# One more pair of heads in flight in sliding-window attention, and the keys' PSUM work issued two to a bank

## The chip, the cores and the metric

The kernel runs on one core of a Trainium2 chip. The metric is the time on the device of one execution, in microseconds; lower is better. The engines that matter are TensorE (PE, with its weight loads as PEld), VectorE (DVE) and ScalarE (ACT). Each takes its own instructions strictly from its own program and waits on semaphores for the others; weights come from HBM through SyncE's DMA queue.

## The reference

The model is a decoder trunk of two layers for 256 tokens of width 2048: an RG-LRU layer, then a sliding-window attention layer with grouped queries, each followed by a SwiGLU. The change is in the second layer alone:

```python
def shared_kv(x, g, w_kv, k_g):
    h = rms_norm(x, g)
    k, v = jnp.split(h @ w_kv, 2, axis=-1)
    k = rms_norm(k.reshape(bsz, s, N_KV_HEADS, HEAD_DIM), k_g)
...
def attn_block(x, g, w_q, q_g, sinks, w_o, k_band, v_band):
    q = rms_norm((h @ w_q).reshape(bsz, s, N_KV_HEADS, GROUP, HEAD_DIM), q_g)
    scores = jnp.einsum("bnqhgd,bnkhd->bnhgqk", q, k_band) * (1.0 / math.sqrt(HEAD_DIM))
    scores = jnp.where(mask, scores, NEG_INF)
    probs = jax.nn.softmax(jnp.concatenate([scores, sink], axis=-1), axis=-1)[..., :-1]
    out = jnp.einsum("bnhgqk,bnkhd->bnqhgd", probs, v_band)
    return x + out.reshape(bsz, s, N_HEADS * HEAD_DIM) @ w_o
```

There are 32 query heads of 64 values and 4 key/value heads; a token sees its own block of 128 tokens up to itself and the part of the block before that lies within 128 tokens.

## The kernel before

**Projections.** Everything is held transposed: features on the partitions, the 256 tokens along the free axis. A weight matrix is cut into tiles of 256 rows by 512 columns. Each tile is a *block* of work (a job): SyncE loads it (`raw`), ScalarE rounds it to `hi` (L243), VectorE takes the rest `lo` (L244), and TensorE multiplies hi by both halves of the activation and lo by the upper half (L281), normally 24 instructions of 256 columns; where two halves are done in one of 512 columns a block has 21. Tiles are loaded four blocks ahead and split three blocks ahead. `group` runs the blocks that add up to four output tiles in four PSUM banks.

**Background work.** All the rest (norms, softmax, copies) is written as generators, which `run_bg` steps between half blocks ("ticks") as far as a budget of VectorE and ScalarE time allows; a `yield n` asks for n ticks' pause. When a block needs an activation that is not yet made, `need` steps the generators until it is there. At most four PSUM banks (`MISC`) are out for background work. The recording layer then places the instructions of each engine, so the order on an engine is not exactly that of the code; the order shown below is the final one.

**Keys.** `kv` projects keys and values. Its task normalises the keys: L704 squares them, L712 sums the squares per head on TensorE (two matmuls, a bank each), L718 to L722 scale, L730 copies each of the four heads' keys to both halves of the partitions through a matmul (a bank each, in turn), and L733 splits the copy into hi and lo as `kd`.

**Attention.** `attn` projects queries in four groups; each group's task makes four *pairs* of heads ready (L959), 16 pairs in all. `pairs` handles them in *turns*, at least `VISIT` = 3 ticks apart. A turn issues on TensorE: the values of pair A (L804, L806: probabilities times V), the six transposes of pair B's probabilities (L814), and the scores of a new pair (L825). Then ScalarE copies the transposes out of PSUM (L895, L896) and the values are split into `at` (L901, by L347 and L348; this is what the output projection reads), and the new pair's softmax follows (`softmax`: VectorE's masked reduction L837, ScalarE's exponentials L851, VectorE's scaling L859). Helpers hold the actual calls, so in the profile ScalarE's work shows as L107 and VectorE's scaling as L125. A pair is thus scored in one turn, transposed in the next and multiplied with the values in the one after.

**Output projection.** L965 multiplies by w_o with `late` = 2: the first two groups run as first six blocks of group 0, first six of group 1, then the last two of each. Block c reads the outputs of pairs 2c and 2c + 1, so pair 11 is first read in the sixth block and pair 15 in the fourteenth.

Of the kernel before, what the change touches and what calls it, by code (L numbers as in the profile page):

```python
# [15 lines left out]
ALU = mybir.AluOpType  # L16

P = 128
D = 2048
T = 256  # L20
DFF = 5632
ND = D // P
NH = DFF // P
HD = 64
EPS = 1e-6
# [10 lines left out]
K_ONE, K_BLK, K_SEL0, K_SEL1, K_ID = 0, 128, 256, 384, 512  # L36
# [12 lines left out]
class Trunk:  # L49
# [470 lines left out]
    def lru(self, gains, rn):  # L520
# [80 lines left out]
        def recur(v):  # L601

            A = lambda s: s[:, 0:T]
            B = lambda s: s[:, T:2 * T]
# [74 lines left out]
    def kv(self, xs, r, gains):  # L679
        nc, con, par = self.nc, self.con, self.par  # L680
        st = {}
        self.kvs = []
        w = self.d["kv"]
        self.kd = [Val() for _ in range(4)]
        self.v = [Val() for _ in range(2)]

        def done(ps):
            k0 = [self.pull((p, False, p)) for p in ps[:2]]
            for b in range(2):
                self.a(self.v[b].ap, ps[2 + b][:, 0:T])  # L690
                self.free_bank(ps[2 + b])

            def task():
                while not self.rv[r].ready:
                    yield 1
                rs = self.rstd[r][:, 0:T]
                for b in range(2):
                    self.ts(self.v[b].ap, self.v[b].ap, self.rstd[r][:, T + b:T + b + 1], None, ALU.mult)
                    self.v[b].ready = True
                    yield  # L700
                sl = [self.slot(F32) for _ in range(2)]
                for j in range(2):
                    self.tt(k0[j], k0[j], rs, ALU.mult)
                    self.a(sl[j][:, 0:T], k0[j], AF.Square)  # L704
                    yield
                yield 1
                p2 = []
                for j in range(2):
                    while not self.room():
                        yield 1  # L710
                    p2.append(self.mbank())
                    nc.tensor.matmul(p2[j][:, 0:T], con[:, K_BLK:K_BLK + P], sl[j][:, 0:T],  # L712
                                     start=True, stop=True)
                yield 1
                for j in range(2):
                    A, B = (sl[j][:, h * T:(h + 1) * T] for h in range(2))
                    m, t = self.nm[:, 0:T], self.nt[:, 0:T]
                    self.ts(m, p2[j][:, 0:T], 1.0 / HD, EPS, ALU.mult, ALU.add)  # L718
                    self.free_mbank(p2[j])
                    self.rsqrt(B, m, t)  # L720
                    self.tt(k0[j], k0[j], B, ALU.mult)
                    self.ts(A, k0[j], par[:, C_GK:C_GK + 1], par[:, C_GQ:C_GQ + 1], ALU.mult, ALU.mult)  # L722
                    yield
                yield 1
                for h in range(4):
                    while not self.room():
                        yield 1
                    p = self.mbank()
                    sel = (K_SEL0, K_SEL1)[h % 2]
                    nc.tensor.matmul(p[:, 0:T], con[:, sel:sel + P], sl[h // 2][:, 0:T],  # L730
                                     start=True, stop=True)
                    yield 1
                    self.split_act(self.kd[h].ap, p[:, 0:T])  # L733
                    self.free_mbank(p)
                    self.kd[h].ready = True
                    yield
                for s in sl:
                    self.free(s)
                for s in k0:
                    self.free_half(s)  # L740
            self.spawn(task())

        for c in range(8):
            def mm(hi, lo, c=c):
                if c == 0:
                    st["ps"] = [self.bank() for _ in range(4)]
                    self.DVE_TICK, self.ACT_TICK, self.SPARE = self.LATER

                    for h in range(4):
                        self.kd[h].ap = self.slot()  # L750
                        self.kvs.append(self.kd[h].ap)
                    s = self.slot(F32)
                    self.kvs.append(s)
                    for b in range(2):
                        self.v[b].ap = s[:, b * T:(b + 1) * T]

                    def more():
                        for k in range(ND):
                            self.gained(k, gains)
                            yield  # L760
                    self.spawn(more())
                ps = st["ps"]
                k0 = 2 * c
                x2 = [self.need(xs[k0 + kt]) for kt in range(2)]
                for f in range(2):
                    for kt in range(2):
                        for high, q in ((1, 0), (1, T), (0, 0)):
                            w0 = (hi if high else lo)[:, kt * 512 + f * P:kt * 512 + f * P + P]
                            nc.tensor.matmul(ps[f][:, 0:T], w0, x2[kt][:, q:q + T],
                                             start=k0 + kt == 0 and high > q, stop=k0 + kt == ND - 1 and not high)  # L770
                self.half_tick()
                for b in range(2):
                    for kt in range(2):
                        k = 2 * c + kt
                        wh, wl = (q[:, kt * 512 + 256:kt * 512 + 512] for q in (hi, lo))
                        xh, xl = (x2[kt][:, q * T + b * P:q * T + b * P + P] for q in range(2))
                        o = ps[2 + b][:, 0:T]
                        nc.tensor.matmul(o, xh, wh, start=k == 0, stop=False)
                        nc.tensor.matmul(o, xh, wl, start=False, stop=False)
                        nc.tensor.matmul(o, xl, wh, start=False, stop=k == ND - 1)  # L780
                for q in x2:
                    self.free(q)
                if c == 7:
                    done(ps)
            self.jobs.append((w[c], mm))

    def attn(self, xs, r, gains, rn):
        nc, con, par = self.nc, self.con, self.par
# [74 lines left out]
        def pairs():  # L863


            A = B = None
            n = 0
            while n < ND or A or B:
                new = None
                if todo and self.kd[todo[0][0] // 4].ready and self.v[0].ready and self.v[1].ready:  # L870
                    new = todo.popleft()
                    n += 1
                elif not (A or B):
                    yield 1
                    continue
                at_tick = self.tick
                count = 2 * bool(A or B) + 2 * bool(new)
                while self.misc + count > self.MISC or len(self.banks) < count or len(self.slots) < 5:
                    yield 1
                pt = [self.mbank() for _ in range(2)] if A or B else None  # L880
                ps = [self.mbank() for _ in range(2)] if new else None
                if A:
                    values(A[0], A[1], pt[1])
                    self.pe(900)
                if B:
                    transposes(B[1], pt)
                    self.pe(700)
                if new:
                    scores(new[0], new[1], ps)
                    self.pe(900)  # L890
                yield 1
                nextA = None
                if B:
                    s = [self.slot(F32) for _ in range(2)]
                    self.a(s[0], pt[0])  # L895
                    self.a(s[1][:, 0:T], pt[1][:, 0:T])  # L896
                    nextA = (B[0], s)
                    yield
                if A:
                    s = self.slot()  # L900
                    self.split_act(s, pt[1][:, T:2 * T])  # L901
                    at[A[0]].ap = s
                    at[A[0]].ready = True
                    yield
                for p in pt or ():
                    self.free_mbank(p)
                A, B = nextA, None
                if new:
                    sc = [self.slot(F32) for _ in range(2)]
                    yield from softmax(new[0], new[2], ps, sc)  # L910
                    B = (new[0], sc)
                yield max(1, at_tick + self.VISIT - self.tick)
            for q in self.kvs:
                self.free(q)
# [145 lines left out]
```

## Time and profile before

| what | before |
|---|---|
| median of three runs | 2011.34 us (2009.05 to 2012.57) |
| the profiled execution: its time | 2007.98 us |
| the profiled execution: its span | 2006.2 us |
| TensorE busy, matmuls | 1988.6 us |
| keys' sums and copies (L712, L730) on TensorE | 1041.4 to 1062.0 us |
| scores (L825) on TensorE | 1071.2 to 1215.3 us |
| values (L804, L806) on TensorE | 1083.6 to 1226.4 us |

A row of the groups of instructions reads: line, engine, operation, written<-read tiles, shape, xcount, then total busy time and mean ns of one, then the idle time ahead of them and who ended it. A row of who waited for whom reads: waiting engine, tile and line <- the one waited for, then us in all, times, longest. A row of the timeline reads: start, duration, instruction, count, and in brackets the idle time ahead of it. A row of the stretches reads: stretch, its length, then busy time (and count) of PE, PEld, DVE, ACT and POOL, granted clock, DMA share and GB/s.

### The profile page before, as it was taken

Reading aid. Unit: us, or ns where it says so; the run is one execution under the profiler, and the core shown is the slowest. Engines: PE = TensorE matmul, PEld = TensorE weight load, DVE = VectorE, ACT = ScalarE, POOL = GpSimd, SP = SyncE. Lnnn points to the kernel's source line nnn. Section 1 sums busy time; section 2 is a strip of 40 time slices with the busy share of each in tenths; the row PEclk is TensorE's granted clock in tenths of the full one; section 3 lists DMA queues with packets and bytes.
Section 4 is the critical chain, followed back from the end, with each engine's and each line's share of the span. In section 5 each row is a group of like instructions: output and inputs, shape, how many; then the busy total and the mean of one; then the engine's idle time right before and its main releaser. Section 6 shows DMA issues by size and latency. Waiting matters only on the chain. (4 is left out here: it accounts for less than half of the span.)

```text
span 2006.2 us, 40340 instructions
## 1 busy us (share of the span) xinstructions
PE 1988.6 (99%) x16843; PEld 1948.9 (97%) x16843; DVE 1275.2 (64%) x2043; ACT 1075.3 (54%) x1619; POOL 0.2 (0%) x4
## 2 busy tenths in 40 slices
PE   9999999999999999999999999999999999999999
PEld 9999999999999999999998889999999999999999
DVE  8989876566556555554677766665566566554443
ACT  7798755454445444443556665554454455444432
POOL 0000000000000000000000000000000000000000
PEclk9999999999999999999999999999999999999999
DMA  7655665666656566655653334656555656666663
GB/s 265 201 188 169 215 193 192 194 196 192 197 191 195 194 193 195 193 191 196 197 182 127 116 117 150 192 189 196 196 192 194 195 191 197 192 196 202 205 206 126
DMA packets 105014, 376.57 MB, mean 188 GB/s; under 512 B 11648, under 2 KB 13824, under 8 KB 104832
## 3 DMA queue, kind: packets, MB, share of 16 engines
q1 hardware_dynamic: 104544, 373.60, 57.6%
q8 instruction: 131, 2.15, 0.4%
q10 hardware_dynamic: 288, 0.40, 0.1%
q14 instruction: 51, 0.42, 0.1%
HBM read 371.86 MB, written 2.10 MB: 186 GB/s over the span
## 5 line engine op out<-in xcount | busy, mean ns | idle before, releaser
L281 PE MATMUL b<-s,hi 128*128 128x256 f32 (+1 forms) x10424 | 1428.2, 283 | 3.5 <-ACT s L107 1.9
L281 PEld LDWEIGHTS b<-s,hi 128*128 128x128 f32 x10424 | 1319.4, 188 | 31.8 <-ACT s L107 2.5
L244 DVE TENSOR_TENSOR lo<-raw,hi 128x1024 fp32r<-128x1024 f32 (+1 forms) x705 | 860.6, 1221 | 666.4 <-ACT hi L243 661.9
L243 ACT ACTIVATE hi<-raw 128x1024 fp32r<-128x1024 f32 (+1 forms) x705 | 745.7, 1059 | 775.6 <-PE b L281 743.0
L281 PE MATMUL b<-s,lo 128*128 128x256 f32 x5504 | 821.2, 276 | 0.0
L281 PEld LDWEIGHTS b<-s,lo 128*128 128x128 f32 x5504 | 714.8, 188 | 0.0
L107 ACT ACTIVATE t<-b 128x256 f32<-128x256 f32 x130 | 48.8, 384 | 59.4 <-PE b L281 38.3
L107 ACT ACTIVATE h<-h 128x256 f32<-128x256 f32 (+1 forms) x104 | 38.8, 375 | 20.9 <-DVE h L116 20.8
L107 ACT ACTIVATE s<-h 128x256 fp32r<-128x256 f32 (+1 forms) x106 | 42.7, 411 | 12.5 <-DVE h L116 10.1
L107 ACT ACTIVATE s<-s 128x256 f32<-128x256 f32 (+1 forms) x112 | 41.0, 417 | 5.5 <-DVE s L120 4.6
L116 DVE TENSOR_TENSOR h<-b,rstd 128x256 f32<-128x256 f32 x100 | 40.9, 414 | 0.0
L107 ACT ACTIVATE s<-x,par 128x256 fp32r<-128x256 f32 x80 | 37.9, 497 | 4.2 <-DVE x L116 3.3
L107 ACT ACT_TABLE_LOAD x31 | 39.8, 1283 | 0.5
L116 DVE TENSOR_TENSOR h<-h,rstd 128x256 f32<-128x256 f32 x94 | 39.0, 419 | 1.5
L116 DVE TENSOR_TENSOR h<-b,t 128x256 f32<-128x256 f32 x92 | 38.2, 417 | 0.0
L120 DVE SCALAR_TENSOR_TENSOR s<-x,par,s 128x256 fp32r<-128x256 f32 x80 | 36.7, 478 | 0.8 <-ACT s L107 0.8
L107 ACT ACTIVATE s<-b 128x256 f32<-128x256 f32 (+2 forms) x64 | 24.7, 435 | 23.0 <-PE b L814 16.7
L116 DVE TENSOR_TENSOR s<-h,s 128x256 fp32r<-128x256 f32 x88 | 36.5, 417 | 0.0
L116 DVE TENSOR_TENSOR h<-h,h 128x256 f32<-128x256 f32 x88 | 36.3, 415 | 0.1
L116 DVE TENSOR_TENSOR s<-s,s 128x256 fp32r<-128x256 f32 (+1 forms) x80 | 31.0, 417 | 5.9 <-ACT s L107 5.8
L837 DVE CUSTOM_DVE_ANT_0 s<-b,con,par 128x128 f32<-128x128 f32 x64 | 27.8, 472 | 6.3 <-PE b L825 6.1
L107 ACT ACTIVATE s<-s,h 128x128 f32<-128x128 f32 x64 | 28.2, 442 | 4.2 <-DVE h L125 4.2
(95 smaller groups left out, 554.5 us busy)
## 6 DMA issues: line engine op xcount, KB each, us to landing
raw<-in_ffn_in SPq DMA_DIRECT2D x352, 512.0 KB, 4.0
raw<-in_ffn_out SPq DMA_DIRECT2D x176, 512.0 KB, 4.2
raw<-in_lru_in SPq DMA_DIRECT2D x63, 512.0 KB, 3.8
raw<-in_lru_out SPq DMA_DIRECT2D x32, 512.0 KB, 3.8
raw<-in_w_q SPq DMA_DIRECT2D x32, 512.0 KB, 3.3
raw<-in_w_o SPq DMA_DIRECT2D x32, 512.0 KB, 3.4
raw<-in_gate SPq DMA_DIRECT2D x8, 512.0 KB, 4.1
raw<-in_kv SPq DMA_DIRECT2D x8, 512.0 KB, 3.3
```

The costliest lines, as they stand in the source:

```text
L107: self.nc.scalar.activation(out, in_, func, **kw)
L116: self.nc.vector.tensor_tensor(out, a, b, op)
L120: self.nc.vector.scalar_tensor_tensor(out, a, s, b, op0, op1)
L243: self.nc.scalar.activation(hi[:, q], raw[:, q], AF.Copy)
L244: self.nc.vector.tensor_tensor(lo[:, q], raw[:, q], hi[:, q].bitcast(F32), ALU.subtract)
L281: self.nc.tensor.matmul(ps[f][0][:, 0:c1 - c0], w, x2[k][:, c0:c1], start=ps[f][2] not in begun, stop=last and all(q[1] != f for q in todo ...
L837: nc.vector.tensor_tensor_reduce(sc[hh][:, c0:c1], ps[hh][:, c0:c1], con[:, K_MASK + c0:K_MASK + c1], rr[:, b * 8 + f * 2 + hh:b * 8 + f * ...
```

## The change

A third place C is put behind B: a pair that is scored goes to C, a turn later to B, and is transposed in the turn after that. So a pair takes four turns in place of three, one more pair is in flight, and `pairs` runs a turn longer. A turn now asks for six free slots of SBUF in place of five. For the keys, the two sums of squares share one PSUM bank; the four copies are issued together into two banks, two to a bank, after a pause of three ticks, and their splits follow one after another.

```diff
-                p2 = []
+                while not self.room():
+                    yield 1
+                p2 = self.mbank()
                 for j in range(2):
-                    while not self.room():
-                        yield 1
-                    p2.append(self.mbank())
-                    nc.tensor.matmul(p2[j][:, 0:T], con[:, K_BLK:K_BLK + P], sl[j][:, 0:T],
+                    nc.tensor.matmul(p2[:, j * T:j * T + T], con[:, K_BLK:K_BLK + P], sl[j][:, 0:T],
                                      start=True, stop=True)
...
+                yield 3
+                while self.misc + 2 > self.MISC or len(self.banks) < 2:
+                    yield 1
+                ps = [self.mbank() for _ in range(2)]
+                for h in range(4):
+                    sel = (K_SEL0, K_SEL1)[h % 2]
+                    nc.tensor.matmul(ps[h // 2][:, h % 2 * T:h % 2 * T + T], con[:, sel:sel + P], sl[h // 2][:, 0:T],
+                                     start=True, stop=True)
                 yield 1
                 for h in range(4):
-                    while not self.room():
-                        yield 1
-                    p = self.mbank()
-                    sel = (K_SEL0, K_SEL1)[h % 2]
-                    nc.tensor.matmul(p[:, 0:T], con[:, sel:sel + P], sl[h // 2][:, 0:T],
-                                     start=True, stop=True)
-                    yield 1
-                    self.split_act(self.kd[h].ap, p[:, 0:T])
-                    self.free_mbank(p)
+                    self.split_act(self.kd[h].ap, ps[h // 2][:, h % 2 * T:h % 2 * T + T])
+                    if h % 2:
+                        self.free_mbank(ps[h // 2])
...
-            A = B = None
+            A = B = C = None
             n = 0
-            while n < ND or A or B:
+            while n < ND or A or B or C:
...
-                elif not (A or B):
+                elif not (A or B or C):
...
-                while self.misc + count > self.MISC or len(self.banks) < count or len(self.slots) < 5:
+                while self.misc + count > self.MISC or len(self.banks) < count or len(self.slots) < 6:
...
-                A, B = nextA, None
+                A, B, C = nextA, C, None
                 if new:
                     sc = [self.slot(F32) for _ in range(2)]
                     yield from softmax(new[0], new[2], ps, sc)
-                    B = (new[0], sc)
+                    C = (new[0], sc)
```

In the changed kernel the lines of `attn` stand two further down: values are L806 and L808, transposes L816, scores L827.

The order of instructions moves at three places that matter below. The first is TensorE in an early turn. In these rows b0 to b7 are the PSUM banks, con_65 the constants (here the identity), and the s are slots; in the kernel before, the turn that does pair 0's values, pair 1's transposes (s39, s41 hold its probabilities) and pair 2's scores (into b5 and b6) stands so:

```order
L804 MATMUL b0_83<-s35_11811,s34_11072 64x256 x2
L806 MATMUL b0_83<-s40_11812,s34_11072 64x128 x2
...
L825 MATMUL b5_88<-s30_11068,s53_11649 128x256
L814 MATMUL b0_83<-con_65,s39_11816 128x128
L814 MATMUL b3_86<-con_65,s39_11816 128x128 x2
L814 MATMUL b0_83<-con_65,s41_11815 128x128
L814 MATMUL b3_86<-con_65,s41_11815 128x128 x2
L825 MATMUL b6_89<-s30_11068,s53_11649 128x256
```

and in the changed kernel the turn with pair 0's values, pair 1's transposes and pair 3's scores so:

```order
L806 MATMUL b5_88<-s41_11893,s34_11072 64x256 x2
L808 MATMUL b5_88<-s39_11894,s34_11072 64x128 x2
L816 MATMUL b5_88<-con_65,s40_11821 128x128
L816 MATMUL b0_83<-con_65,s40_11821 128x128 x2
L816 MATMUL b5_88<-con_65,s35_11820 128x128
L816 MATMUL b0_83<-con_65,s35_11820 128x128 x2
L827 MATMUL b6_89<-s30_11068,s31_11663 128x128
L827 MATMUL b7_90<-s30_11068,s31_11663 128x128
```

The transposes stood among the scores, behind nine of the twelve; now they stand between values and scores.

The second place is TensorE at the sixth block of w_o. Before, pair 11's values (into b4) stand two blocks and a half ahead of the block that reads its output, slot s10:

```order
L281 MATMUL b2_85<-s1_12466,hi2_77 128x256 x4
L804 MATMUL b4_87<-s39_12999,s34_11072 64x256 x2
L806 MATMUL b4_87<-s53_13000,s34_11072 64x128 x2
L281 MATMUL b7_90<-s1_12466,hi2_77 128x256 x4
...
L281 MATMUL b2_85<-s20_13003,hi1_76 128x256 x4
L281 MATMUL b7_90<-s20_13003,hi1_76 128x256 x4
L281 MATMUL b2_85<-s10_13067,hi1_76 128x256 x4
```

and now (values into b5, output in slot s33, with pair 13's twelve scores between):

```order
L281 MATMUL b0_83<-s49_13043,lo0_79 128x256 x2
L806 MATMUL b5_88<-s55_13110,s34_11072 64x256 x2
L808 MATMUL b5_88<-s26_13111,s34_11072 64x128 x2
L827 MATMUL b6_89<-s9_11071,s15_12920 128x128
...
L281 MATMUL b7_90<-s51_13114,hi1_76 128x256 x4
L281 MATMUL b0_83<-s51_13114,hi1_76 128x256 x4
L281 MATMUL b7_90<-s33_13167,hi1_76 128x256
L281 MATMUL b0_83<-s33_13167,hi1_76 128x256
L281 MATMUL b1_84<-s1_11984,hi2_77 128x256 x3
```

Values and reader have moved together, and the reader is followed by three matmuls of another block, put there ahead of the rest of s33's.

The third place is ScalarE's program at the same point. Before, the copy of pair 11's output from b4 stands ahead of three weight splits, the table load and the exponentials of pair 12 (h6 holds that pair's sums):

```order
L107 ACTIVATE s10_13067<-b4_87 128x256
L243 ACTIVATE hi2_77<-raw2_73 128x1024
L243 ACTIVATE hi3_78<-raw3_74 128x1024
L243 ACTIVATE hi0_75<-raw0_71 128x1024
L107 ACT_TABLE_LOAD
L107 ACTIVATE h6_101<-h6_101 128x4
```

and now (the output of pair 11 in s33, that of pair 10 in s51):

```order
L107 ACTIVATE s51_13114<-b4_87 128x256
L243 ACTIVATE hi0_75<-raw0_71 128x1024
L107 ACT_TABLE_LOAD
L107 ACTIVATE h6_101<-h6_101 128x4
L107 ACTIVATE s21_13117,h6_101<-s21_13117,h6_101 128x128
L107 ACTIVATE s21_13117,h6_101<-s21_13117,h6_101 128x256
L107 ACTIVATE s22_13118,h6_101<-s22_13118,h6_101 128x128
L107 ACTIVATE s22_13118,h6_101<-s22_13118,h6_101 128x256
L107 ACTIVATE s33_13167<-b5_88 128x256
```

The copy has moved from ahead of the split, the load and the exponentials to behind them.

More of the change, by code (lines that the diff above doesn't have):

```diff
@@ L717, in task @@
                     m, t = self.nm[:, 0:T], self.nt[:, 0:T]
-                    self.ts(m, p2[j][:, 0:T], 1.0 / HD, EPS, ALU.mult, ALU.add)
-                    self.free_mbank(p2[j])
+                    self.ts(m, p2[:, j * T:j * T + T], 1.0 / HD, EPS, ALU.mult, ALU.add)
+                    if j:
+                        self.free_mbank(p2)
                     self.rsqrt(B, m, t)
```

## The prediction

> **What bounds the kernel now.** First the page: its span, the busy row of TensorE and the granted clock.
>
> ```profile
> span 2006.2 us, 40340 instructions
> PE 1988.6 (99%) x16843; PEld 1948.9 (97%) x16843; DVE 1275.2 (64%) x2043; ACT 1075.3 (54%) x1619; POOL 0.2 (0%) x4
> PEclk9999999999999999999999999999999999999999
> ```
>
> TensorE is busy nearly all the time and its clock is never cut, so only time in which TensorE stands still, or work taken off it, can shorten the run. 2006.2 - 1988.6 = 17.6 us of standing still is all there is in the matmul records. So the second view is the table of who waited for whom, of matmuls (PE) and of weight loads (PEld), in the stretch 1035 to 1240 us in which the change works:
>
> ```profile
> PE b L814 <- DVE s L125: 9.7, 11, 1.0
> PEld b L814 <- DVE s L125: 12.2, 12, 1.3
> PEld b L825 <- issue: 2.5, 15, 0.2
> ```
>
> The only matmuls that stand still there are the transposes of the probabilities (L814): 11 times they wait for VectorE's last scaling of the softmax (L125), 9.7 us in all, and 12.2 us by the weight loads. The third view, TensorE's instructions in order of time, tells which figure is the loss:
>
> ```profile
> 1065.52 1.10 PE L281 MATMUL b<-s,lo 128*128 128x256 f32 x8
> 1066.46 1.57 PE L281 MATMUL b<-s,hi 128*128 128x256 f32 x12
> ...
> 1078.88 0.75 PE L281 MATMUL b<-s,hi 128*128 128x256 f32 x5
> 1080.60 0.88 PE L814 MATMUL b<-con,s 128*128 128x128 f32 x6 [0.98 <-DVE s L125]
> 1081.23 1.54 PE L281 MATMUL b<-s,hi 128*128 128x256 f32 x11
> ```
>
> Eight matmuls of 256 columns take 1066.46 - 1065.52 = 0.94 us from start to start, 0.1175 us each. The five from 1078.88 should thus have let the transposes start at 1079.47; they started at 1080.60. That is 1.13 us lost where the matmul record says 0.98, because the modelled end of a matmul overlaps what follows. 12.2 / 11 = 1.11 agrees with 1.13, so I take 12.2 us as the loss and keep 9.7 as its lower bound.
>
> The Trainium skill, page "Perfetto Trace Analysis", section "Identifying the Most-Contended Engine", says that matmul busy time is a poor measure for a pipelined TensorE and that the busy share of the weight loads should be read in its place. By the matmul wait alone the sum below would be 2.5 us smaller; the start times just read agree with the page.
>
> **The change, part by part.** *Transposes two turns behind.* Before, a turn transposes the pair whose scores stood one turn earlier; now it transposes the pair of two turns earlier. By the order of the changed kernel, pair 0 has 69 matmul rows of L281 between its scores and its transposes, where it had 50, and most later pairs more. The work between is a whole turn of other pairs, so all of VectorE's scalings for a pair are queued ahead of the next pair's last reduction. That takes away up to the whole loss: **-12.2 us** (bounds -9.7 and -12.2).
>
> What is late next? The tightest are pairs 0 and 4, the first of their groups.
>
> ```profile
> 1071.16 0.95 PE L825 MATMUL b<-s,s 64*128 64x128 f32 x12
> 1072.05 2.15 PE L281 MATMUL b<-s,hi 128*128 128x256 f32 x13
> ...
> L837 DVE CUSTOM_DVE_ANT_0 s<-b,con,par 128x128 f32<-128x128 f32 x32 | 13.0, 406 | 6.3 <-PE b L825 6.1
> L837 DVE DVE_READ_ACCUMULATOR2_ANT h<- 128x1 f32 x64 | 5.3, 83 | 0.0
> ```
>
> Pair 0's scores started at 1071.16 and its probabilities were ready at 1080.60, 9.44 us later. In the new order of VectorE one more score reduction of pair 1 stands ahead of pair 0's scalings, 0.406 + 0.083 = 0.49 us: ready after 9.93. TensorE gets there after two sets of scores (1072.05 - 1071.16 = 0.89 each), 69 rows of L281 of which three are 512 wide (so 72 x 0.1175 = 8.46) and two entries of 0.1 each: 10.4 us. The margin is 0.5 us for each of the two pairs. As VectorE can be a little late I put **+0.3 us** for both together (bounds 0 and 1.0).
>
> *A turn more at the end.* The output projection L965 reads the attention outputs in order; pairs now finish a turn later, while its blocks stand where they stood. In the order shown above, the values of pair 11 stood some 70 matmuls of L281 ahead of the ones that read them; now their block follows pair 11's values and pair 13's scores directly, with 8 matmuls between. And ScalarE's copy of that output (L347) now stands behind a weight split, a table load and the exponentials of pair 12. The trace has the same queue for the same pair in the old kernel:
>
> ```profile
> 1191.36 0.96 PE L825 MATMUL b<-s,s 64*128 64x128 f32 x12
> 1192.24 2.15 PE L281 MATMUL b<-s,hi 128*128 128x256 f32 x16
> ...
> 1194.48 1.06 ACT L243 ACTIVATE hi<-raw 128x1024 fp32r<-128x1024 f32 x1 [2.84 <-PE b L281]
> 1195.56 1.28 ACT L107 ACT_TABLE_LOAD   x1
> 1196.85 0.21 ACT L107 ACTIVATE h<-h 128x4 f32<-128x4 f32 x1
> ...
> 1198.72 1.04 ACT L243 ACTIVATE hi<-raw 128x1024 fp32r<-128x1024 f32 x1
> ```
>
> The split waits for TensorE to have read the buffer that it overwrites (16 matmuls from 1192.24 end their starts at 1194.12; it begins 0.36 us later), then come the load (1.28 us) and the exponentials, and ScalarE is free at 1198.72, 7.36 us after the start of pair 12's scores. The copy behind them and the values' own time:
>
> ```profile
> L107 ACT ACTIVATE s<-b 128x256 fp32r<-128x256 f32 x16 | 6.2, 388 | 3.6 <-PE b L806 3.6
> ...
> 1203.89 0.65 PE L804 MATMUL b<-s,s 128*64 128x256 f32 x4
> 1204.37 0.39 PE L806 MATMUL b<-s,s 128*64 128x128 f32 x4
> 1204.69 0.84 PE L825 MATMUL b<-s,s 64*128 64x128 f32 x9
> ```
>
> The copy ends at 7.36 + 0.39 = 7.75 us. TensorE, counted from the same start: pair 12's scores 0.89, 24 matmuls 2.82, an entry 0.1, values 1204.69 - 1203.89 = 0.80, pair 13's scores 0.89, 8 matmuls 0.94: 6.44 us. So it waits 7.75 - 6.44 = **+1.3 us** at this block (bounds: 0 if the split finds its buffer free earlier, 2.4 if one more split of 1.06 us stands in the way). VectorE's half of that output is wanted five matmuls later and follows within 0.5 us of the copy, which five matmuls (0.59 us) cover. At pair 15 the same thing happens without a softmax in the queue: the split ahead of the copy begins 0.36 us after the sixteenth of the block's 24 matmuls, so 0.58 before the values start, and ends 0.3 before they do, the copy ends 0.39 us after them, and four matmuls (0.47 us) cover it; I cost this at nothing.
>
> The Trainium skill, page "ScalarE: Activation LUTs", section "What ACT_TABLE_LOAD costs", puts a switch of tables at 1.28 us for the load and some 1.4 us for a drain. Here the load starts 0.02 us after the split ends and the next activation starts as the load ends (1195.56 + 1.28 = 1196.84), so this trace has the load and no drain. With the drain the wait of 1.3 would be 2.7 us and the whole gain 1.4 us smaller.
>
> *Fewer entries.* Where TensorE goes from the projection to attention work a little is lost:
>
> ```profile
> 1111.52 1.10 PE L281 MATMUL b<-s,lo 128*128 128x256 f32 x8
> 1112.55 0.95 PE L825 MATMUL b<-s,s 64*128 64x128 f32 x12
> 1113.44 2.15 PE L281 MATMUL b<-s,hi 128*128 128x256 f32 x16
> ```
>
> Eight matmuls of 0.94 us, yet 1.03 to the next start: 0.09 us. The order has 39 such entries before and 29 after (scores and transposes now stand behind the values in one run, and the keys' four copies in one place where they had four). Ten times 0.09 is 0.9; some of these small gaps reappear inside the longer runs, so **-0.8 us** (bounds 0 and -1.0).
>
> *The keys.* The same two sums and four copies are multiplied, so TensorE does no less; none of them is among the waits above, before or behind. The first scores come 11 matmuls (1.3 us) later than they did. TensorE has the projection to do meanwhile, and thirteen blocks of w_o stand ahead of the first that reads the last pair, so this costs nothing by itself; it is part of why the end is tight. The sixth slot asked for (six free in place of five) only moves turns, which the order already contains.
>
> Sum: -12.2 + 0.3 + 1.3 - 0.8 = **-11.4 us**. The profiled execution took 2007.98 us, 1.78 more than its span, so its like would take 1996.6. The median of the three runs, 2011.34, lies 3.36 above it; the same 11.4 from the median gives **1999.9 us**.
>
> **The rivals.**
>
> ```profile
> L107 ACT ACTIVATE s<-b 128x512 f32<-128x512 f32 x16 | 9.5, 591 | 0.0
> L107 ACT ACTIVATE s<-b 128x256 f32<-128x256 f32 x22 | 8.2, 378 | 17.1 <-PE b L814 16.7 <-PE b L281 0.3
> L107 ACT ACT_TABLE_LOAD x7 | 9.0, 1283 | 0.1
> ...
> 1070.00:1230.00 160.00, 150.26 (x1283) 135.27 (x1282) 109.20 (x360) 105.85 (x274) 0.00 (x0) 1.00 0.36 116
> ```
>
> 1. *The wait moves to the values.* Values need the two copies of the transposes, 0.591 + 0.378 = 0.97 us. If they took the place of the wait in 12 turns, 11.6 us come back: 2011.5, no change. Against it: transposes and values stand at least 24 matmuls (2.8 us) apart in the new order, and ScalarE, which today waits 16.7 us for late transposes, gets them sooner.
>
> 2. *The distance is eaten.* If VectorE's queue, not the place of the transposes, sets when probabilities are ready, half of the loss stays: -6.1 + 1.3 - 0.8 = -5.6, 2005.7. For it: the margin of pairs 0 and 4 is only 0.5 us. Against it: most later pairs have values and transposes of other pairs in between as well, and VectorE is busy 109.2 of 160 us.
>
> 3. *Slower: ScalarE's queue starves the first w_o blocks.* Around the sixth block of w_o the reader's need drives the turns, one of them only 24 matmuls long: 2.82 + 0.80 + 0.63 + 0.89 = 5.1 us of TensorE, while ScalarE has in it the split 1.06, a table load 1.28, exponentials 1.87 (1198.72 - 1196.85), two copies 0.97 and the output's copy 0.39: 5.6 us. If it falls behind in that way for all five pairs 11 to 15, each block waits. It decides from 2.5 us a block (12.5 in place of 1.3 eats the 11.4); at 3.4 us, 17 us, the run takes 2011.34 - 12.7 + 17 = 2015.6. Against it: the other turns have 36 to 48 matmuls, and in the whole stretch ScalarE is busy 105.85 of 160 us.
>
> **How the numbers follow.** Forecast 0.75, rival 1 0.10, rival 2 0.10, rival 3 0.05. The bounds of the terms give a gain of 9.7 - 2.4 - 1.0 = 6.3 to 12.2 + 1.0 = 13.2 us, so 1998.1 to 2005.0; the runs shown lie 2.3 below and 1.2 above their median, and with rival 2 (2005.7) inside, the range is 1995.8 to 2006.9. It leaves out rivals 1 and 3. A measurement of this kernel tells about 0.2%, 4 us, from no change: faster by more than that 0.85, within it 0.10, slower 0.05.
>
> **What would show it.** In the new profile the weight loads of the transposes (now L816) should wait at most 1 us in all for VectorE, down from 12.2; one matmul of L281 near 1190 us should wait about 1.3 us for ScalarE; the span should be near 1995 us. If the values (L806) or the scores wait, rival 1 holds; if transposes wait still, rival 2; if L281 waits for ScalarE at several blocks in 1180 to 1240, rival 3.

## The result, and the profile after

| what | before | after |
|---|---|---|
| median of three runs | 2011.34 us (2009.05 to 2012.57) | 2000.18 us (1997.12 to 2000.57) |
| the profiled execution: its time | 2007.98 us | 1997.12 us |
| the profiled execution: its span | 2006.2 us | 1995.3 us |

The ratio is 0.9942, with a 95% interval of 0.9919 to 0.9964: about 11 us faster. The page of the kernel after, the same three rows as before:

```profile
span 1995.3 us, 40349 instructions
PE 1985.8 (100%) x16843; PEld 1947.2 (98%) x16843; DVE 1274.7 (64%) x2043; ACT 1073.6 (54%) x1619; POOL 0.2 (0%) x4
PEclk9999999999999999999999999999999999999999
```

The same 16843 matmuls run, at the same uncut clock. TensorE's standing still fell from 17.6 to 1995.3 - 1985.8 = 9.5 us, and its busy time by 2.8 us; that fits modelled ends of matmuls that reach into the wait behind them. Who waited for whom from 1035 to 1240 us in the kernel after, first the matmuls' rows, then those of the weight loads (us in all, times, longest):

```profile
PE b L281 <- ACT s L107: 1.0, 1, 1.0
PE b L281 <- DVE h L839: 0.3, 1, 0.3
```

```profile
PEld b L827 <- issue: 1.9, 11, 0.2
PEld b L816 <- issue: 1.5, 9, 0.2
PEld b L281 <- ACT s L107: 1.2, 1, 1.2
PEld b L281 <- DVE h L839: 0.9, 2, 0.5
PEld b L816 <- DVE h L116: 0.3, 2, 0.2
```

No row of a transpose for VectorE's scaling (L125) is left. Two waits stand there that the kernel before did not have: one matmul of L281 waits for ScalarE, and the weight loads of L281 wait 0.9 us for VectorE's masked reductions (L839).

**Where to measure.** All of the difference lies in one stage. The view of one line's instructions gives its first and last start; of before, the first projection of the keys and the norm's sum behind w_o:

```profile
L769 PE MATMUL b<-s,hi x64: 276/278/363, 1015.5 to 1037.0; 128*128 128x256 f32 x64
L396 PE MATMUL b<-acc,con x8: 378/378/483, 34.4 to 1296.9; 128*128 128x256 f32 x8
```

and of after:

```profile
L771 PE MATMUL b<-s,hi x64: 276/278/363, 1015.5 to 1037.0; 128*128 128x256 f32 x64
L396 PE MATMUL b<-acc,con x8: 378/378/483, 34.5 to 1286.0; 128*128 128x256 f32 x8
```

From 1015.5 to the last L396 the kernel before takes 281.4 us and the kernel after 270.5: 10.9 us, the whole difference of the spans. Behind it both have 709.3 us left. Below, this is called **the stage**. It is a finer measure than the median, because what lies ahead of it takes about 3 us more in some executions (last section): the stage begins at 1015.5 to 1016.3 us in half of the fourteen profiled executions that are compared here and at 1018.5 to 1018.9 in the other half, whatever was changed behind. The runs of one kernel differ by as much: 1997.12, 2000.57 and 2000.18 us for the kernel after.

### The profile page after: what moved, and what is told of

Its sections match the earlier page's. It is cut to its first block, busy times and chain, and to the rows that moved or that the text cites. A ratio compares the mean times of both kernels' runs of the same rounds, so it can differ in the third digit from the quotient of the medians.

```text
span 1995.3 us, 40349 instructions
## 1 busy us (share of the span) xinstructions
PE 1985.8 (100%) x16843; PEld 1947.2 (98%) x16843; DVE 1274.7 (64%) x2043; ACT 1073.6 (54%) x1619; POOL 0.2 (0%) x4
## 3 DMA queue, kind: packets, MB, share of 16 engines
q8 instruction: 131, 2.15, 0.4%
## 5 line engine op out<-in xcount | busy, mean ns | idle before, releaser
L281 PE MATMUL b<-s,hi 128*128 128x256 f32 (+1 forms) x10424 | 1426.4, 283 | 5.1 <-ACT s L107 2.9
L281 PEld LDWEIGHTS b<-s,hi 128*128 128x128 f32 x10424 | 1318.1, 188 | 33.9 <-ACT s L107 3.4
L281 PE MATMUL b<-s,lo 128*128 128x256 f32 x5504 | 820.0, 276 | 0.0
L281 PEld LDWEIGHTS b<-s,lo 128*128 128x128 f32 x5504 | 714.3, 188 | 0.0
L107 ACT ACTIVATE s<-h 128x256 fp32r<-128x256 f32 (+1 forms) x106 | 42.7, 411 | 12.2 <-DVE h L116 9.9
L116 DVE TENSOR_TENSOR h<-b,rstd 128x256 f32<-128x256 f32 x100 | 40.9, 415 | 0.0
L116 DVE TENSOR_TENSOR h<-h,rstd 128x256 f32<-128x256 f32 x94 | 39.0, 420 | 1.5
L116 DVE TENSOR_TENSOR h<-b,t 128x256 f32<-128x256 f32 x92 | 38.2, 417 | 0.0
L116 DVE TENSOR_TENSOR s<-h,s 128x256 fp32r<-128x256 f32 x88 | 36.5, 417 | 0.0
L116 DVE TENSOR_TENSOR h<-h,h 128x256 f32<-128x256 f32 x88 | 36.3, 415 | 0.0
L116 DVE TENSOR_TENSOR s<-s,s 128x256 fp32r<-128x256 f32 (+1 forms) x80 | 30.4, 419 | 5.3 <-ACT s L107 5.2
L116 DVE TENSOR_TENSOR x<-x,b 128x256 f32<-128x256 f32 x64 | 25.1, 415 | 9.8 <-PE b L281 9.8
```

The costliest lines, as they stand in the source:

```text
L107: self.nc.scalar.activation(out, in_, func, **kw)
L116: self.nc.vector.tensor_tensor(out, a, b, op)
L281: self.nc.tensor.matmul(ps[f][0][:, 0:c1 - c0], w, x2[k][:, c0:c1], start=ps[f][2] not in begun, stop=last and all(q[1] != f for q in todo ...
```

## The experiments

The theory: the gain is the distance between a pair's scores and its transposes, and the pair in flight is only the means; the price is the wait at w_o's sixth block. The rivals: the keys' part does it, or fewer changes of work on TensorE do, or the executions differ for another reason. Each kernel below was timed beside the kernel before on its own chip. "Waits" is the sum of all rows of the weight loads' waits from 1035 to 1240 us, "entries" the number of places where TensorE passes from the projection to attention or key work, by the order. "Rest" is the change of the stage less the change of the waits. Where starts are spoken of, it is the time from the start of one matmul to the start of the next, by the timeline.

| kernel | ratio to before (95%) | stage us | waits us | rest us | entries |
|---|---|---|---|---|---|
| before | 1 | 281.4 | 16.1 | | 39 |
| after | 0.9942 (0.9919 to 0.9964) | 270.5 | 6.6 | -1.4 | 29 |
| after_again | 0.9944 (0.9930 to 0.9958) | 270.5 | 6.6 | -1.4 | 29 |
| keys_alone | 0.9984 (0.9975 to 0.9993) | 278.6 | 13.7 | -0.4 | 38 |
| pairs_alone | 0.9947 (0.9934 to 0.9960) | 270.2 | 6.1 | -1.2 | 33 |
| no_pause | 0.9935 (0.9921 to 0.9949) | 270.2 | 6.1 | -1.2 | 30 |
| tick_later | 0.9960 (0.9947 to 0.9974) | 271.9 | 6.7 | -0.1 | 47 |
| three_turns | 0.9939 (0.9927 to 0.9952) | 268.6 | 5.2 | -1.9 | 29 |
| visit_2 | 0.9938 (0.9926 to 0.9950) | 268.7 | 4.4 | -1.0 | 30 |
| late_3 | 0.9937 (0.9920 to 0.9953) | 268.6 | 5.3 | -2.0 | 29 |

Further down come four more, here with stage, waits, rest and entries: pause_alone (278.5, 13.7, -0.5, 41), keys_no_pause (282.0, 16.2, +0.5, 36), no_pause_visit_2 (269.0, 4.3, -0.6, 31) and three_turns_visit_2 (271.7, 7.3, -0.9, 32).

**One part at a time.** keys_alone keeps the keys' part and takes the third place away; pairs_alone is the kernel before with the third place and the old keys.

```diff
# keys_alone, against after
-                A, B, C = nextA, C, None
+                A, B = nextA, None
...
-                    C = (new[0], sc)
+                    B = (new[0], sc)
# pairs_alone, against before: the same lines the other way round
```

> Theory 1 (the whole gain is the end of the transposes' wait for VectorE; the keys' part is worth nothing by itself): the transposes go on waiting, 7 to 13 us by the weight loads, and the time is that of before, ratio 0.998 to 1.002. Theory 2 (the keys' copies, issued in one place, carry part of the gain): ratio 0.996 to 0.999 with the transposes' wait unchanged at about 12 us.

> Theory 1: no transpose waits for a scaling. The scores start 11 matmuls earlier than with the keys' part, by the order pair 11's values then stand 36 matmuls ahead of the sixth block of w_o, and the wait of 1.2 us there goes; also that of the new group's banks for a score reduction (0.9 us). Span 1992.5 to 1995, ratio 0.993 to 0.9945. Theory 2 (the keys' part carries some of the gain): span 1997 to 2003.

pairs_alone has the whole gain: its stage is 11.2 us shorter than that of before, and no transpose waits for VectorE. So the third place does it. But keys_alone isn't nothing: its stage is 2.8 us shorter. Its weight loads' waits:

```profile
PEld b L816 <- DVE s L125: 10.3, 10, 1.3
PEld b L827 <- issue: 2.0, 12, 0.2
PEld b L281 <- issue: 0.9, 5, 0.2
```

The row of L125 counts ten waits in place of twelve. The two parts don't add: -2.8 and -11.2 make -10.9 together, because with the third place there is no wait of a transpose left that the keys' part could take away.

pairs_alone lacks the wait at w_o's sixth block, as expected, but its span of 1998.2 us is not the 1992.5 to 1995 that I expected; it lies in the range of theory 2. About 3 us are its stage's start (1018.7 us). The rest is a wait that was not foreseen, in TensorE's order of time at the hand-over from the third to the fourth group of queries:

```profile
1132.76 0.87 PE L281 MATMUL b<-s,hi 128*128 128x512 f32 x3
1134.04 0.97 PE L281 MATMUL b<-s,hi 128*128 128x256 f32 x6 [0.42 <-ACT s L107]
1135.71 0.74 PE L281 MATMUL b<-s,hi 128*128 128x256 f32 x4 [0.70 <-ACT s L107]
```

The first block of the new group is to write PSUM banks from which ScalarE is still copying the previous group's queries; 1.8 us by the weight loads.

**The pause, and the kernel after once more.** Ahead of the keys' copies the change has a longer pause. no_pause shortens it in the kernel after.

```diff
-                yield 3
+                yield 1
```

> The whole change, but one tick in place of three ahead of the keys' copies, which stand together two to a bank. Theory 1: the pause is what makes the end tight, so this is as fast as the pairs' part alone, span 1992.5 to 1995, without the wait at the sixth block of w_o. If the copies standing together is what delays the scores: a wait of about 1 us is there still and the span is 1995 to 1996.

> The changed kernel once more, beside the others on the same chip: ratio 0.993 to 0.996, span near 1995.3, one wait of 1 to 1.3 us of L281 for ScalarE at the sixth block of w_o, none of a transpose for a scaling.

after_again repeats the stage to 0.1 us, with the same waits; as far as one repeat tells, differences of the stage of 0.3 us and more are differences of the programs. no_pause has lost the wait at the sixth block, as expected, but at 1995.2 us its span is not below 1995: it has pairs_alone's stage, 270.2 us, and pairs_alone's waits at the same hand-over, not after's. Between these two kernels stand all sums and copies of the keys, in the new form and in the old, at the same pace of turns. They make 0.0 us here.

**The pause alone.** Then the 2.8 us of keys_alone should come from the pause, which delays the first turn, and not from sums and copies that share banks. pause_alone is the kernel before with `yield 3` in place of `yield 1` ahead of the copies; keys_no_pause is keys_alone with the pause put back to one tick.

```diff
# pause_alone, against before
-                yield 1
+                yield 3
# keys_no_pause, against keys_alone
-                yield 3
+                yield 1
```

> The kernel before with three ticks in place of one ahead of the keys' copies, which stay one to a bank in four places. By the order its attention then stands exactly as with the whole keys' part alone. If the keys' part helped by moving the turns (theory 1): the transposes wait 10.3 us by the weight loads, and from the first key projection to the fourth norm it takes 278.6 us to 279 us, as with the keys' part alone, against 281.4 before. If it helped by its copies standing together: 281.4.

> The keys' part alone, without the longer pause: copies and sums together, two to a bank; the attention stands as before. Theory 1: 281.1 to 281.4 us from the first key projection to the fourth norm, the transposes wait 12.2 us as before (three entries fewer at 0.09 us are all there is to gain). Rival (copies together carry the gain): 278.6.

The row of pause_alone's transposes:

```profile
PEld b L814 <- DVE s L125: 10.3, 10, 1.3
```

It is keys_alone's row, and the stage is 278.5 us against 278.6. keys_no_pause has the 12.2 us of before again and a stage of 282.0 (ratio 1.0009, 1.0000 to 1.0019), 0.6 above before and above the 281.1 to 281.4 expected. Its waits are those of before (16.2 us against 16.1). What differs is the pace at which TensorE starts its matmuls. One block near the end of the stage, in before:

```profile
1217.02 1.98 PE L281 MATMUL b<-s,hi 128*128 128x256 f32 x16
1218.83 1.07 PE L281 MATMUL b<-s,lo 128*128 128x256 f32 x8
```

and the same block in keys_no_pause:

```profile
1220.12 2.05 PE L281 MATMUL b<-s,hi 128*128 128x256 f32 x16
1222.01 1.10 PE L281 MATMUL b<-s,lo 128*128 128x256 f32 x8
```

Sixteen matmuls take 1.81 us from start to start in the one, 0.113 each, and 1.89 in the other, 0.118 each. Both paces occur in the stage of every kernel. Of the 256-column matmuls of L281 that follow each other there without a wait, 566 stand 0.113 us apart in before and 418 in keys_no_pause; 148 times 0.0045 us is 0.7 us, which is the difference. What sets the pace is open (last section).

So the pause is all of the keys' part that takes waits away, 1.9 of its 2.8 us by the row of L125, and it does so by where the turns fall.

**Distance without a pair in flight.** tick_later keeps two places, but issues the new pair's scores first and the transposes a tick (half a block) later.

```diff
# against before; the scores of the new pair now stand ahead of this
-                if B:
-                    transposes(B[1], pt)
-                    self.pe(700)
...
+                if B:
+                    yield 1
+                    transposes(B[1], pt)
+                    self.pe(700)
```

> The kernel before, with the transposes half a block (12 matmuls, 1.4 us) after values and scores in the same turn: no pair more in flight. Theory 1 (a wait of 1.1 us a turn, so any work of 1.4 us put ahead covers it): the transposes' wait falls from 12.2 to at most 4 us. Values and readers come closer in the forced turns at w_o (7 to 10 rows behind what they need), which costs 2 to 5 us there: span 1996 to 2002. Rival (the softmax gets later by as much as the transposes do): they wait 8 us or more, span 2003 to 2008.

```profile
PEld b L814 <- DVE s L125: 1.8, 2, 1.2
PEld b L281 <- ACT s L107: 1.5, 4, 0.5
```

One tick of distance takes away 10.4 of the 12.2 us of that row, with no further pair in flight. The stage, 271.9 us, is only 1.4 us behind that of the kernel after, although TensorE is entered 47 times in place of 29. What gained was the distance, as the prediction had it.

**More distance.** three_turns puts a fourth place behind C, with eight free slots asked for.

```diff
-                A, B, C = nextA, C, None
+                A, B, C, E = nextA, C, E, None
...
-                    C = (new[0], sc)
+                    E = (new[0], sc)
```

> Transposes three turns behind the scores (a fourth place, eight slots asked for). Theory 1 (two turns already cover the whole softmax): no gain more, transposes wait 0 to 0.5 us as in the changed kernel; the end is one turn tighter, so L281 waits 1 to 3 us at the w_o blocks; span 1994.5 to 1998. Rival (part of the wait is still hidden in what the changed kernel shows as issue time of the transposes, 1.5 us): that goes too and the span is 1993 to 1994.

I expected the wait at the sixth block to grow to 1 to 3 us; it is gone, and the stage is 1.9 us shorter than after's. The span, 1993.7 us, lies in the rival's range, but not for the rival's reason: the rows of issue of the transposes didn't go, they grew from 1.5 to 2.1 us. Of the 1.9 us 1.2 are the wait at the sixth block, and 0.6 are TensorE's pace (611 matmuls of L281 stand 0.113 us apart, 487 in after). ScalarE's order of time there:

```profile
1185.98 1.06 ACT L243 ACTIVATE hi<-raw 128x1024 fp32r<-128x1024 f32 x1 [1.79 <-issue]
1187.69 0.39 ACT L107 ACTIVATE s<-b 128x256 fp32r<-128x256 f32 x1 [0.65 <-PE b L808]
1188.41 0.40 ACT L107 ACTIVATE s<-s,h 128x128 f32<-128x128 f32 x1 [0.34 <-DVE h L125]
```

The copy of pair 11's output (1187.69) stands ahead of the exponentials, not behind them. How many turns a pair takes doesn't set this wait; what stands ahead of the copy in ScalarE's program does.

**Moving the turns against the blocks.** visit_2 lets turns follow each other after two ticks, no_pause_visit_2 has the short pause as well, and three_turns_visit_2 has the fourth place. late_3 leaves the turns and starts w_o with its first two groups' first five blocks, so that pair 11 is read later and pair 15 earlier.

```diff
# visit_2, against after; also in no_pause_visit_2 and three_turns_visit_2
-    VISIT = 3
+    VISIT = 2
# late_3, against after
-        self.project(self.d["w_o"], ND, at, gains, rn, late=2)
+        self.project(self.d["w_o"], ND, at, gains, rn, late=3)
```

> The changed kernel with turns at least two ticks apart in place of three. Theory 1: the transposes still have two turns, 66 matmuls or more, and do not wait; the pairs finish two blocks earlier, so no block of w_o waits for ScalarE: span 1992.5 to 1994.5. Rival (closer turns pile up VectorE's and ScalarE's queues): transposes or values wait 2 us or more, span 1996 to 2000.

> Both: one tick ahead of the keys' copies and turns two ticks apart. Theory 1: the waits that are left in the stretch are only those of entering (issue, 3 to 4 us by the weight loads); span 1992.5 to 1994.5, no better than either alone by more than 0.5 us. Rival as for the two ticks alone: 1996 to 2000.

> The changed kernel with the last three blocks of w_o's first two groups held back in place of two, so that pair 11's output is first read five blocks later. Theory 1: the wait of 1.0 us (1.2 by the weight loads) at the sixth block goes. Pair 15's output is read a block earlier, 12 matmuls after the transposes that it needs, with two copies (0.97 us), the values and its own copy in between: 0.5 to 2 us of wait there. 269.3 to 271.3 us from the first key projection to the fourth norm (270.5 in the changed kernel).

> Transposes three turns behind and turns two ticks apart. Theory 1: nothing is left to gain, since either alone has no wait of a transpose, of values or of w_o; 268.4 to 269.2 us from the first key projection to the fourth norm, plus up to 1.8 us if the third group's banks are handed over as late as in the kernels whose first scores start earlier.

In visit_2 no row of L281 is left but one of issue, and its stage is 268.7 us; its span of 1996.6 is above the 1992.5 to 1994.5 expected, since its stage begins late, at 1018.6. no_pause_visit_2 has a stage of 269.0 (ratio 0.9940, 0.9927 to 0.9952). In late_3 the wait at the sixth block is gone and the 0.9 us for L839 stay, as its weight loads show:

```profile
PEld b L827 <- issue: 1.7, 10, 0.2
PEld b L816 <- issue: 1.5, 9, 0.2
PEld b L281 <- DVE h L839: 0.9, 2, 0.5
```

The new wait of 0.5 to 2 us at pair 15 that I expected did not come: pair 15 has room to spare. The stage is 268.6 us, below the 269.3 to 271.3 expected and 1.9 below after's; 1.2 of that is the wait, and 0.6 again the pace (625 against 487). three_turns_visit_2 was to join two gains and joined none: 271.7 us (0.9958, 0.9943 to 0.9973), a little above the 268.4 to 271.0 expected. Two waits for ScalarE, 1.7 us together, and one of 0.6 for VectorE stand at its hand-over to the fourth group, the place where pairs_alone and no_pause wait.

The best kernels here, three_turns, late_3 and visit_2, are 1.8 to 1.9 us shorter than after by the stage. Their ratios, 0.9937 to 0.9939, lie inside after's interval, so the medians alone don't tell them from it.

## Why the prediction was right, point by point

The forecast was 1999.9 us and the median is 2000.18. The profiled execution fell by 10.9 us where the sum said 11.4. The two waits that carry the argument, the one that goes and the one that comes, are where the prediction put them. That the total came so near is in part luck: the largest term is about 1.3 us too large, a wait of 0.9 us was left out, and the entries' term is too small by about as much. The 0.3 us between forecast and median are luck altogether, as runs of the same kernel differ by 3 us.

1. **The transposes, -12.2.** The mechanism is right: no row of L816 for L125 is left, and tick_later shows that distance alone removes 10.4 us of it. The size is too large. 12.2 us is the sum of twelve rows of the weight loads, not of the eleven by which the prediction divided it to confirm its 1.13 us. And it holds what a transpose behind other attention work costs without any such wait: in the kernel after, twelve of the sixteen sets of transposes still have 0.17 us each (L816 for issue 1.5, for L116 0.3, for L131 0.2). By the starts, the eleven stalls of before cost 10.9 us, once 0.20 us is taken off behind attention work and 0.12 behind the projection (0.24 behind the one matmul of 512 columns), which is what such a step takes where nothing is waited for. Four stalls stood behind the projection, as the one that the prediction read, and cost 1.04 to 1.17 us; seven stood behind scores and cost 0.85 to 1.01. So neither row is the loss: 9.7 is too small and 12.2 too large.

2. **The first pairs, +0.3.** It was 0. Pair 0's scores and transposes on TensorE in the kernel after,

```profile
1072.70 0.96 PE L827 MATMUL b<-s,s 64*128 64x128 f32 x12
...
1083.25 0.81 PE L816 MATMUL b<-con,s 128*128 128x128 f32 x6
```

   and its probabilities' scaling on VectorE:

```profile
1080.05 1.00 DVE L125 TENSOR_SCALAR s<-s,h 128x128 f32<-128x128 f32 x4
```

   TensorE came 10.55 us after the scores' start (forecast 10.4), the probabilities were there after 1081.05 - 1072.70 = 8.35 (forecast 9.93). The margin is 2.2 us, not 0.5. The 9.44 us from the kernel before were too long a base: there VectorE began with pair 0's scores 2.9 us after their start (1074.07 against 1071.16), behind work for the queries' norm, and in the kernel after 1.0 us (1073.70 against 1072.70). Pair 4, the other tight one, is ready at 1119.76 + 1.01 = 1120.77 for transposes at 1122.22, a margin of 1.45 us:

```profile
1119.76 1.01 DVE L125 TENSOR_SCALAR s<-s,h 128x128 f32<-128x128 f32 x4
...
1122.22 0.82 PE L816 MATMUL b<-con,s 128*128 128x128 f32 x6
```

3. **The sixth block of w_o, +1.3.** Right in place, mechanism and size. TensorE in the kernel after (pair 12's scores first, then pair 13's):

```profile
1181.63 0.96 PE L827 MATMUL b<-s,s 64*128 64x128 f32 x12
...
1186.34 0.95 PE L827 MATMUL b<-s,s 64*128 64x128 f32 x12
1187.22 1.21 PE L281 MATMUL b<-s,hi 128*128 128x256 f32 x8
1189.40 1.57 PE L281 MATMUL b<-s,hi 128*128 128x256 f32 x11 [0.97 <-ACT s L107]
```

   and ScalarE:

```profile
1184.75 1.06 ACT L243 ACTIVATE hi<-raw 128x1024 fp32r<-128x1024 f32 x1 [2.08 <-issue]
1185.83 1.28 ACT L107 ACT_TABLE_LOAD   x1
1187.12 0.20 ACT L107 ACTIVATE h<-h 128x4 f32<-128x4 f32 x1
...
1188.98 0.36 ACT L107 ACTIVATE s<-b 128x256 fp32r<-128x256 f32 x1
```

   Eight matmuls from 1187.22 should have led on at 1188.16; the next starts at 1189.40, 1.24 us late, when ScalarE has done the split, the load, the exponentials and then the copy, ending at 1189.34. Counted from the start of pair 12's scores, as in the prediction, the copy ended after 7.71 us (forecast 7.75) and TensorE was there after 6.53 (forecast 6.44). The activation after the load starts 0.01 us after it ends (1185.83 + 1.28 = 1187.11). The Trainium skill, page "ScalarE: Activation LUTs", section "What ACT_TABLE_LOAD costs", adds a drain of some 1.4 us to the load; here too it is not seen, and the wait is the 1.3 without it, not the 2.7 with it.

4. **Fewer entries, -0.8.** Too small, and not the whole cause. The waits fell by 16.1 - 6.6 = 9.5 us and the stage by 10.9, so by the waits 1.4 us are left to this term, above the bound of 1.0. By the starts it is more: -10.9 for the transposes' stalls, +1.6 for two new stalls of L281 (1.1 at the sixth block, 0.5 at the hand-over of point 6) and +0.5 for a slower pace (487 matmuls 0.113 us apart against 566) leave -2.1.

   One part of it is seen in the rows. Besides the 0.09 us on entering, TensorE loses 0.1 on coming back: sixteen matmuls of L281 read 2.15 us behind scores (1192.24 in the prediction) and 2.05 at the same pace elsewhere (1220.12 in keys_no_pause). The prediction counted the first loss alone. But the number of entries doesn't order the kernels: no_pause has three fewer than pairs_alone and the same rest, keys_no_pause three fewer than before, pause_alone two more. With stalls and pace taken off, the starts leave 0.1 us to keys_no_pause, 1.6 to keys_alone and pause_alone, 1.2 to tick_later and 2.0 to 2.6 to the kernels with a third or fourth place. That goes rather with how often the transposes stand in the middle of a pair's scores: seven times in before and keys_no_pause, three times in keys_alone and pause_alone, never in the others. No run changed that alone, or the entries alone, so what the rest is made of is argued, not shown.

5. **The keys, 0.** Right inside this change: 0.0 between no_pause and pairs_alone. Wrong as a statement on the part: by itself it gives 2.8 us, through its pause, as the transposes of the shifted turns wait less for their probabilities (10.3 us against 12.2). The step that failed was to count only what the copies cost and not the turns that the pause moves.

6. **Left out: the hand-over of banks, +0.9.** The prediction had no term for it. TensorE where the fourth group of queries begins in the kernel after,

```profile
1126.79 1.32 PE L281 MATMUL b<-s,hi 128*128 128x512 f32 x5
1128.40 1.22 PE L281 MATMUL b<-s,hi 128*128 128x256 f32 x8 [0.29 <-DVE h L839]
```

   and VectorE:

```profile
1126.67 0.41 DVE L839 CUSTOM_DVE_ANT_0 s<-b,con,par 128x128 f32<-128x128 f32 x1
...
1127.80 0.54 DVE L839 CUSTOM_DVE_ANT_0 s<-b,con,par 128x256 f32<-128x256 f32 x1
1128.27 0.09 DVE L839 DVE_READ_ACCUMULATOR2_ANT h<- 128x1 f32 x1
```

   The new group's block gets banks that held a pair's scores until VectorE's last reduction at 1128.27. In pairs_alone and no_pause the same hand-over meets ScalarE and costs 1.8 us; in visit_2 it costs nothing. By the starts the two costs are 0.5 and 1.4 us.

By the waits the account is -12.2 + 1.0 (sixth block, beside 0.2 that L281 waited for ScalarE before) + 0.9 (banks) + 0.1 (issue: 3.6 us against 3.5) + 0.7 (rows of 0.2 and 0.3) = -9.5, and -1.4 of point 4: -10.9. Of the rivals none came: the values don't wait (1), no transpose waits for L125 (2), and L281 waits for ScalarE at one block of w_o, not five (3).

## What to carry to other kernels

When the bound engine waits for a result, ask first how much work of others must stand between its maker and its reader: here half a block took away 10.4 of the 12.2 us of the row, and a further item in flight the rest. The sum of such a row is not yet the loss; the distance between the starts is, less what the same step takes where nothing waits (10.9 us here). A deeper pipeline moves its last items against whoever reads them, so read, for each late result, what stands ahead of its last copy in that engine's program, and which banks a new group is given; those two places and TensorE's pace make up most of the 3 us by which the variants with a third place differ. And measure a change in its own stage: what lies ahead of it varied here by as much.

## What the runs showed of the hardware that was not expected

TensorE works at two paces at a full granted clock, early in the program, in code that no kernel here changes. The view of stretches for the kernel after (stretch, length, busy time and count of PE, then PEld, DVE, ACT, POOL, clock, DMA share, GB/s):

```profile
60.00:80.00 20.00, 20.00 (x179) 20.00 (x178) 18.44 (x37) 11.87 (x17) 0.00 (x0) 1.00 0.59 190
100.00:150.00 50.00, 50.00 (x435) 49.63 (x434) 43.29 (x80) 45.96 (x80) 0.00 (x0) 1.00 0.58 185
200.00:300.00 100.00, 100.00 (x839) 98.25 (x838) 78.79 (x132) 65.24 (x110) 0.00 (x0) 1.00 0.63 202
```

and for visit_2:

```profile
60.00:80.00 20.00, 20.00 (x173) 20.00 (x172) 17.21 (x34) 10.76 (x16) 0.00 (x0) 1.00 0.56 186
100.00:150.00 50.00, 50.00 (x423) 49.62 (x422) 42.90 (x79) 43.58 (x75) 0.00 (x0) 1.00 0.56 180
200.00:300.00 100.00, 100.00 (x838) 98.25 (x838) 78.80 (x133) 65.22 (x108) 0.00 (x0) 1.00 0.64 208
```

TensorE is busy throughout in both, the clock reads 1.00 in both, and yet the one starts 179 and 435 matmuls where the other starts 173 and 423, about 3% more. Between 40 and 100 us its matmuls of 256 columns stand 0.113 us apart in the kernel after and 0.118 in visit_2. The 300th matmul of the program starts at 43.5 and 43.6 us, the 1200th at 146.9 and 150.4; from 200 us to the stage the two agree. This is where the 3 us come from by which these profiled executions differ ahead of the stage. That it is also what separates the runs of one kernel is not shown, and the cause stays open; no run was made for it.

The same two paces are in the stage itself. There, a stretch at the shorter distance towards its end begins about 15 us earlier in before than in keys_no_pause, and 17 to 20 us earlier in late_3 and three_turns than in after. So a part of what a change does in its stage, up to 0.9 us here, is in no row of waits.
